# Memory values by tokens: the last four memory-projection tiles of a decode step computed with the tokens stationary, norm weights applied on ScalarE, and cache pages staged later

## The chip, the cores and the metric

The kernel runs on one core of a Trainium2 chip. The metric is the device time of one execution in microseconds; three executions of the kernel before took 619.06, 621.07 and 621.22 us (median 621.07).

The names used below: TensorE (PE in the profile) does the matmuls, PEld is its weight load; VectorE is DVE, ScalarE is ACT, GpSimd is POOL, and SP is the engine that only issues transfers. SP and POOL issue nearly all transfers here; each engine works in the order in which its instructions were written.

## The reference, cut to what matters

One layer of a decoder for 256 prompt tokens and 8 x 4 sampled tokens, all in float32.

```python
def rms_norm(x, g):
    y = xf * lax.rsqrt(jnp.mean(xf * xf, axis=-1, keepdims=True) + NORM_EPS)
    return y * g
...
# memory: 256 tokens x 2048, projected to keys (4 heads x 128) and values (4 heads x 128)
mkv = (rms_norm(mem_prompt, mem_norm_g) @ w_mem_kv).reshape(1, 256, 2, 4, 128)
...
h = rms_norm(x, norm_g)                       # 288 tokens in all
c_h, c_b, c_c, c_g, q, n_g, b_g, kv6, m_q, m_g = split_cols(h @ w_in)
# group A: gated convolution; group B: 8 query heads over compressed, selected and sliding-window
# keys, for the sampled tokens read from 16 cache pages per sequence; group M: attention of m_q
# over the memory keys and values
return x + concatenate([y_a, y_b, y_m]) @ w_out    # and a final rms_norm; mkv is an output too
```

## The kernel before

**Layout and products.** Activations lie with features on the 128 partitions and tokens along the free axis: `x` is 16 planes of 128 x 288, the memory `m` 16 planes of 128 x 256. Every projection runs output tile by output tile: `product` takes a tile of 128 output features, with the weights as stationary operand and the tokens as moving one (matmuls of 256 or 288 columns). A weight tile comes as two halves of 128 x 1024, numbered `s` through the whole program. Float32 accuracy is got from two reduced-precision parts: ScalarE writes a half's high part (`wh`), VectorE its low part (`wl` = `w` - `wh`), and each of the 8 blocks of a half costs three matmuls (high x high, high x low, low x high): 24 in a half, 48 in a tile. `w_hi(s + 2)` and `w_lo(s + 1)` are written when half `s` begins, and `w_load` fetches half `s + 6` near its end into one of five buffers.

**The memory stage.** The 1024 memory columns are 8 tiles: keys are tiles 0 to 3, values 4 to 7. Tiles 0 and 1 go through `first_tiles` on unsplit weights, tiles 2 to 7 through `product` with 256 columns. The reciprocal norms of the tokens (`rstd_m`, held in `Vc`) come late, so they multiply the results. The values are needed with tokens on the partitions, so each value tile is multiplied into `mvt` by VectorE, stored by POOL, and transposed: two transposes into `mvtp` on TensorE and two copies into `mixed` by ScalarE (`mem_rstd`).

**Preparing x.** `x` comes in six pieces `rx` (five of three planes, one of one). `prep_x` multiplies each plane by its norm weights and by the tokens' `rstd_x` on VectorE, three instructions to a piece; ScalarE then writes the piece's high part and VectorE its low part, `x`.

**The cache stream.** Pages are loaded by SP into six buffers `st` as these come free, in one fixed order: compressed pages (`ckc`, multiplied on VectorE and POOL and summed into `pooled`), and in between groups of four tiles of selected keys (`ckk`), which TensorE uses at once (`sk`), later values (`od`). A planner places each use where its own estimate says that the data is there. `window_copies` has POOL issue 16 copies of 512 KB from memory to memory (`o_wk`, `o_wv`), one every `T_WIN[1]` ticks; a tick is half of a weight half. `ON_SYNC` is the half from which weights are issued by POOL and not by SP.

The order of all instructions is written by the program: generators are advanced at every tick by `chunk`. In the profile line L118 is every matmul, L123 every transpose, L135 every VectorE and ScalarE operation.

Of the kernel before, what the change touches and what calls it, by code (L numbers as in the profile page):

```python
# [55 lines left out]
T_MK, T_K1, T_MV, T_V1 = (111, 117), (165, 204), (230, 240), (259, 271)  # L56
T_WIN = (20, 31)
T_LAST = 4
# [6 lines left out]
X_AT = (16, 17)  # L65
ON_SYNC = 14
KV_ORDER = (2, 4, 3, 5, 0, 1)
# [10 lines left out]
def decode_step(ctx, tc, xT, xN, xD, memT, cst, w_in, w_mem, w_out, w_bg, pt, ptv, ckc, ckk, ckv, wk, wv, mk, mv,  # L78
                o_y, o_kv, o_mem, o_conv, o_wk, o_wv):
    nc = tc.nc  # L80
# [163 lines left out]
    def product_half(out, hi, lo, first, last):  # L244
        s = nhalf[0]
        nhalf[0] += 1
        w_hi(s + 2)
        w_lo(s + 1)
        wh, wl = his.pop(s), los.pop(s)
        mm = []  # L250
        for j in range(8):
            a = wh[:, j * 128:(j + 1) * 128]
            mm += [(j, a, hi(j)), (j + (0 if s > DIRECT + 1 else 4), a, lo(j)), (j + 8, wl[:, j * 128:(j + 1) * 128], hi(j))]
        mm.sort(key=lambda x: x[0])
        for n, (_, a, b) in enumerate(mm):
            if s == DIRECT and n == 0:
                w_load(s + WR)
            if n == LOAD_AT:
                w_load(s + WR + 1)
                next(x_next, None)  # L260
            matmul(out, a, b, start=(first and n == 0), stop=(last and n == 23))
            if n == 23 and LOW_FIRST <= s < NH - 18:
                w_lo(s + 2)
            if n % 12 == 11 and not (last and n == 23):
                chunk()
# [3 lines left out]
    def first_tiles():  # L269


        z = [pz.tile([128, 512], F32, name=f"zf{i}", tag="z")[:, :256] for i in range(2)]
        for k0 in (0, 8):
            for i in range(2):
                s = nhalf[0]
                nhalf[0] += 1
                w_hi(s + 2)
                w_lo(s + 1)
                w = raws[s]
                for j in range(8):  # L280
# [470 lines left out]
    for i in range(3):  # L751
# [28 lines left out]

    x_next = x_loads()

    w_load(0)
# [78 lines left out]
    def mem_rstd():  # L862
# [6 lines left out]
        yield 3  # L869
        yield from token_rstd(rstd_m, [macc[:, 0:256]], 256, 1)  # L870
        env["rstd_m"] = True
        for i in range(8):
            while i not in mem_raw:
                yield 1
            dst = mem_raw[i]
            if i < 4:
                vec.tensor_tensor(dst, dst, rstd_m, op=ALU.mult)
            yield 1
            if i == 3:
                nc.gpsimd.dma_start(o_mem[0:4].rearrange("m p n -> p m n"), mkT)  # L880
# [11 lines left out]
    def token_rstd(dst, planes, n, lag):  # L892

# [7 lines left out]
        yield lag  # L901
        r = small(3, "yr")
        w = len(groups)
# [10 lines left out]
    def prep_x():  # L914

        g, r = C("ng"), rstd_x
# [17 lines left out]
    def sum_x():  # L934
# [24 lines left out]
        nc.sync.dma_start(wbg, w_bg)  # L959
        yield 2  # L960
        for t in buffers:
# [38 lines left out]
    def mem_tile(i, z):  # L1000
        dst = mkT[:, i, :] if i < 4 else zt("A", "mvt")[:, :256]
        if i < 4:
            act.activation(dst, z, AF.Copy)
        else:
            yield 2
            assert "rstd_m" in env
            vec.tensor_tensor(dst, z, rstd_m, op=ALU.mult)
        mem_raw[i] = dst

# [529 lines left out]


def _inputs(x_prompt, x_sample, cache_kv, cache_win, state_conv, cache_mem, page_table, mem_prompt,
            norm_g, w_in, w_conv, a_cmp, w_cmp, mem_norm_g, w_mem_kv, w_out, final_g):
# [33 lines left out]
                memT=A(np.concatenate([vec(mem_norm_g), tr(mem_prompt.reshape(256, D)).reshape(128, KT * 256)], 1)), cst=A(cst), w_in=A(_ktiles(wcat)),  # L1576
                w_mem=A(_ktiles(w_mem_kv[0])), w_out=A(_ktiles(wo)), w_bg=A(wbg), pt=A(pt), ptv=A(ptv), ckc=A(ckc), ckk=A(ckk), ckv=A(ckv),
                wk=A(wk), wv=A(wv), mk=A(mk), mv=A(mv))


_OUTS = dict(o_y=(128, KT, NT), o_kv=(12, 128, NT), o_mem=(8, 128, 256), o_conv=(128, 72), o_wk=(4, 2, 128, 1024),
             o_wv=(2, 4, 128, 1024))


def _outputs(r):
# [9 lines left out]
            A(kv[:NTP, 4:6])[None, None], A(conv[0:2])[None, None],  # L1595
            A(r["o_mem"].reshape(2, 4, 128, 256).transpose(3, 0, 1, 2))[None, None],
            A(kv[NTP:, 0:4]).reshape(1, 8, 4, 4, 2, 128), A(win)[None], A(conv[2:18]).reshape(1, 8, 2, 512))
# [15 lines left out]
```

## Time and profile before

| | |
|---|---|
| median of three executions | 621.07 us (619.06 to 621.22) |
| the profiled execution | 622.86 us, its span 620.4 us |
| PE busy | 601.8 us (97% of the span) |
| DVE, ACT, POOL busy | 458.0 (74%), 286.3 (46%), 203.5 us (33%) |
| moved by transfers | 188.40 MB, mean 304 GB/s |

The profiled execution is 1.79 us above the median. Its span leaves 2.46 us of its time around it. Busy time on PE counts overlapping matmuls once; in the timeline view, whose rows give the start, the duration, the engine, the line and the operation, the start of one row and the start of the next say how long the first held the engine.

### The profile page before, as it was taken

Reading aid. Unit: us, or ns where it says so; the run is one execution under the profiler, and the core shown is the slowest. Engines: PE = TensorE matmul, PEld = TensorE weight load, DVE = VectorE, ACT = ScalarE, POOL = GpSimd, SP = SyncE. Lnnn points to the kernel's source line nnn. Section 1 sums busy time; section 2 is a strip of 40 time slices with the busy share of each in tenths; the row PEclk is TensorE's granted clock in tenths of the full one; section 3 lists DMA queues with packets and bytes.
Section 4 is the critical chain, followed back from the end, with each engine's and each line's share of the span. In section 5 each row is a group of like instructions: output and inputs, shape, how many; then the busy total and the mean of one; then the engine's idle time right before and its main releaser. Section 6 shows DMA issues by size and latency. Waiting matters only on the chain.

```text
span 620.4 us, 13332 instructions
## 1 busy us (share of the span) xinstructions
PE 601.8 (97%) x4893; PEld 557.0 (90%) x4893; DVE 458.0 (74%) x737; ACT 286.3 (46%) x500; POOL 203.5 (33%) x282
## 2 busy tenths in 40 slices
PE   8999999999899999999999999999999999999993
PEld 5998999999699998988898888888989889999993
DVE  4789899979395689978978788969586442447764
ACT  4855545444355434335334444344534453446650
POOL 2022545434235334323474522323113434122200
PEclk9999999999999999999999999999999999999997
DMA  8999799999889998978888798899988989578723
GB/s 307 408 406 396 262 329 307 320 314 339 293 264 371 350 408 319 360 278 281 297 288 303 246 375 285 280 345 303 360 296 326 329 283 336 169 252 286 234 89 152
DMA packets 74929, 188.40 MB, mean 304 GB/s; under 512 B 8752, under 2 KB 26064, under 8 KB 74608
## 3 DMA queue, kind: packets, MB, share of 16 engines
q0 software_dynamic: 26048, 100.48, 46.1%
q1 hardware_dynamic: 47664, 85.11, 38.6%
q10 hardware_dynamic: 1152, 1.97, 0.8%
q8 instruction: 38, 0.62, 0.4%
q14 instruction: 27, 0.22, 0.1%
HBM read 182.31 MB, written 13.60 MB: 316 GB/s over the span
## 4 chain that ended last, share of the span: by engine, by line
PE 77%; DVE 10%; DMA 8%; issue 2%; ACT 1%; SPq 0%; ACTq 0%; DVEq 0%
PE z L118 59%; PE od L118 3%; DMA st<-ckk 3%; PE sk L118 3%; DMA st<-ckc 3%; DVE pooled L135 2%; PE zf L118 2%; DVE wl L135 2%; PE acc L118 2%; DMA rx<-xT 2%; PE s L118 2%; DMA mraw<-memT 1%; DVE st L135 1%; PE pt L123 1%; DVE ysum L135 1%
## 5 line engine op out<-in xcount | busy, mean ns | idle before, releaser
L118 PE MATMUL z<-x,wh 128*128 128x288 f32 x1664 | 254.2, 302 | 0.4 <-ACT wh L135 0.4
L135 DVE TENSOR_TENSOR wl<-w,wh 128x1024 fp32r<-128x1024 f32 x148 | 183.9, 1243 | 93.0 <-PE z L118 41.6
L118 PEld LDWEIGHTS z<-x,wh 128*128 128x128 f32 x1664 | 229.4, 188 | 9.2 <-issue 6.9
L135 ACT ACTIVATE wh<-w 128x1024 fp32r<-128x1024 f32 x148 | 154.8, 1052 | 15.8 <-PE z L118 11.7
L118 PE MATMUL z<-x,wl 128*128 128x288 f32 x832 | 127.1, 295 | 0.6 <-DVE wl L135 0.6
L118 PEld LDWEIGHTS z<-x,wl 128*128 128x128 f32 x832 | 115.7, 188 | 0.8 <-DVE wl L135 0.8
L350 POOL TENSOR_TENSOR st<-st,cst 128x512 f32<-128x512 f32 x56 | 62.8, 1121 | 132.9 <-issue 68.2
L219 POOL DMA_DIRECT2D w<-w_in x104 | 58.4, 562 | 91.5 <-DVE wl L135 74.7
L135 DVE TENSOR_REDUCE pooled<-st 128x16 f32<-128x1024 f32 x56 | 67.8, 1210 | 3.4 <-POOL st L350 3.3
L135 DVE TENSOR_TENSOR st<-st,cst 128x512 f32<-128x512 f32 x56 | 40.1, 715 | 4.6 <-DMA st<-ckc 4.3
L572 POOL DMA_INDIRECT st<-ckv,rows_v x29 | 31.2, 1077 | 29.9 <-PE od L118 16.8
L219 POOL DMA_DIRECT2D w<-w_out x32 | 17.5, 550 | 60.1 <-DVE wl L135 43.0
L118 PE MATMUL z<-y,wh 128*128 128x288 f32 x256 | 37.0, 297 | 0.0
L118 PE MATMUL z<-y1a,wh 128*128 128x288 f32 x224 | 35.2, 298 | 0.0
L118 PEld LDWEIGHTS z<-y,wh 128*128 128x128 f32 x256 | 35.1, 188 | 0.0
L118 PEld LDWEIGHTS z<-y1a,wh 128*128 128x128 f32 x224 | 31.5, 188 | 1.6 <-issue 0.8
L118 PE MATMUL z<-m,wh 128*128 128x256 f32 x192 | 27.3, 287 | 0.5 <-DVE mvt L135 0.5
L135 ACT ACTIVATE P<-P,nm 128x128 f32<-128x128 f32 (+1 forms) x32 | 14.2, 445 | 28.1 <-DVE nm L135 28.1
L118 PEld LDWEIGHTS z<-m,wh 128*128 128x128 f32 x192 | 24.7, 191 | 0.8 <-issue 0.7
L118 PE MATMUL sk<-st,qz 128*32 128x256 f32 x288 | 20.5, 382 | 2.5 <-DMA st<-ckk 2.5
L135 ACT ACTIVATE ysum<-z 128x288 f32<-128x288 f32 x16 | 6.6, 413 | 34.1 <-PE z L118 34.1
L118 PE MATMUL z<-y,wl 128*128 128x288 f32 x128 | 19.6, 295 | 0.0
(284 smaller groups left out, 696.4 us busy)
## 6 DMA issues: line engine op xcount, KB each, us to landing
w<-w_in POOLq DMA_DIRECT2D x104, 512.0 KB, 6.4
st<-ckc SPq DMA_DIRECT2D x112, 256.0 KB, 6.5
w<-w_out POOLq DMA_DIRECT2D x32, 512.0 KB, 5.0
st<-ckk SPq DMA_DIRECT2D x112, 128.0 KB, 4.7
w<-w_mem SPq DMA_DIRECT2D x13, 512.0 KB, 7.8
o_wk<-wk POOLq DMA_DIRECT2D x8, 512.0 KB, 6.0
o_wv<-wv POOLq DMA_DIRECT2D x8, 512.0 KB, 6.9
qk<-ckc SPq DMA_DIRECT2D x16, 256.0 KB, 5.4
```

Source lines behind the costliest of these rows:

```text
L118: nc.tensor.matmul(out, a, b, **kw)
L123: nc.tensor.transpose(out, a, b)
L135: return getattr(self.engine, name)(*args, **kw)
L219: (nc.gpsimd if s >= ON_SYNC else nc.sync).dma_start(raws[s], wsrc[s])
L350: done.append(eng.tensor_tensor(tm[:, :, kv], tm[:, :, kv], acmp[:, kv].unsqueeze(1).unsqueeze(1).to_broadcast([128, 2, 4, 64]), op=ALU.mu ...
L572: nc.gpsimd.indirect_dma_start(t, None, ckv, bass.IndirectOffsetOnAxis(ap=rows_v[:, j * 4 + b:j * 4 + b + 1], axis=0))
```

## The change

The four value tiles become `mem_values`: two output tiles `zv0`, `zv1` of 128 tokens x 512 features. The stationary operand is a block of 128 memory tokens (high or low part), the moving one 512 columns of weights, so the matmuls have 512 columns and the result already lies by tokens. The value weights are laid out for it on the host. A token's reciprocal norm is then one number on its partition (`mr`), which ScalarE applies as it copies the result from PSUM; transposes, `mvt` and its copies go. `x`'s norm weights are applied by ScalarE, plane by plane, four halves after the piece was asked for; VectorE then multiplies a whole piece by `rstd_x` in one instruction. `STAGE_AT` lets the pages begin at tick 22 and no sooner (before: 19), `T_WIN` has the copies begin at tick 33 with 30 ticks between (before: 20 and 31), and `ON_SYNC` goes from 14 to 19. `run_half` holds what was the loop of `product_half`.

```diff
-T_WIN = (20, 31)
+T_WIN = (33, 30)
-ON_SYNC = 14
+STAGE_AT = 22
+ON_SYNC = 19
...
+    def run_half(s, mm, last, between=None):
+        m = len(mm) // 2
+        for n, (out, a, b, start, stop) in enumerate(mm):
...
+            if n == LOAD_AT * m // 12:
                 w_load(s + WR + 1)
                 next(x_next, None)
+                if s > 5:
+                    next(x_scale, None)
+            matmul(out, a, b, start=start, stop=stop)
...
+            if n == 7 and between:
+                between()
...
+    def mem_values():
+        z = [pz.tile([128, 512], F32, name=f"zv{tt}", tag="z") for tt in range(2)]
+
+        def out(tt):
+            planes = mixed[:, 12 + 2 * tt:14 + 2 * tt, 0:256]
+            act.activation(planes, z[tt].rearrange("p (a n) -> p a n", a=2), AF.Copy, scale=mr[:, tt:tt + 1])
+            nc.gpsimd.dma_start(o_memv[tt].rearrange("p (a n) -> p a n", a=2), planes)
+
+        for h in range(8):
...
+            for tt in range(2):
+                for k in range(2):
+                    hi, lo = (m_hl[n][:, 2 * h + k, tt * 128:(tt + 1) * 128] for n in range(2))
+                    w = slice(k * 512, (k + 1) * 512)
+                    early = 2 * tt + (k if h == 7 and tt else 0)
+                    mm += [(early, tt, hi, wh[:, w]), (early, tt, lo, wh[:, w]), (2.5 if h == 7 and not tt else 4, tt, hi, wl[:, w])]
...
+        out(1)
...
+    def x_scales():
+        for i in range(6):
+            yield
+            k, t = xg[i]
+            for j in range(t.shape[1] // NT):
+                act.activation(xr[k + j], xr[k + j], AF.Copy, scale=C("ng")[:, k + j:k + j + 1])
...
     def mem_rstd():
...
-            if i >= 4:
-                nc.gpsimd.dma_start(o_mem[i], dst)
-                yield 2
-                t = ptr.tile([128, 512], F32, name=f"mvtp{i}", tag="t")
-                for s in range(2):
-                    transpose(t[:, s * 128:(s + 1) * 128], dst[:, s * 128:(s + 1) * 128], ident)
-                for s in range(2):
-                    act.activation(mvn(s, i - 4), t[:, s * 128:(s + 1) * 128], AF.Copy)
...
     def prep_x():
-                for j in range(k, k + n):
-                    vec.scalar_tensor_tensor(xr[j], xr[j], g[:, j:j + 1], r, op0=ALU.mult, op1=ALU.mult)
+                xv = x.rearrange("p (k n) -> p k n", n=NT)
+                vec.tensor_tensor(xv, xv, r.unsqueeze(1).to_broadcast([128, n, NT]), op=ALU.mult)
...
     def mem_tile(i, z):
-            yield 2
-            assert "rstd_m" in env
-            vec.tensor_tensor(dst, z, rstd_m, op=ALU.mult)
...
-    for i in range(2, 8):
+    for i in range(2, 4):
         then(mem_tile(i, proj(*m_hl, 256)))
+    mem_values()
```

In the instructions the change shows at three places. A name's first number is the half (`w13`) or the tile, the number behind the underscore only tells one use from another.

TensorE in the middle of the value tiles. Before, tile 6 (`z12`, weight half 12), with the two transposes of tile 4 among its matmuls:

```order
L118 MATMUL z12_600<-m1_111,wh12_512 128x256
L118 MATMUL z12_600<-m0_110,wh12_512 128x256
L118 MATMUL z12_600<-m1_111,wh12_512 128x256
L123 MATMUL mvtp4_617<-cst_90,mvt_507 128x128 x2
L118 MATMUL z12_600<-m0_110,wh12_512 128x256
L118 MATMUL z12_600<-m1_111,wh12_512 128x256
L118 MATMUL z12_600<-m0_110,wh12_512 128x256
L118 MATMUL z12_600<-m1_111,wh12_512 128x256
L118 MATMUL z12_600<-m0_110,wl12_558 128x256 x8
```

Now, the second part of one half and the beginning of the next, on the two token tiles:

```order
L119 MATMUL zv1_426<-wh10_427,m0_110 128x512
L119 MATMUL zv1_426<-wh10_427,m1_111 128x512
L119 MATMUL zv0_425<-wl10_460,m0_110 128x512 x2
L119 MATMUL zv1_426<-wl10_460,m0_110 128x512 x2
L119 MATMUL zv0_425<-wh11_458,m0_110 128x512
L119 MATMUL zv0_425<-wh11_458,m1_111 128x512
L119 MATMUL zv0_425<-wh11_458,m0_110 128x512
L119 MATMUL zv0_425<-wh11_458,m1_111 128x512
```

A half is 12 matmuls of 512 columns where it was 24 of 256, and the transposes are gone. In all, 192 matmuls of 256 columns and 8 transposes go and 96 matmuls of 512 come; every other matmul stays.

VectorE from the moment that both sets of reciprocal norms are there. Before (`mixed` is a key tile, `Vc` the norms):

```order
L135 TENSOR_TENSOR mixed_95<-mixed_95,Vc_99 128x256 x2
L135 SCALAR_TENSOR_TENSOR rx0_247<-rx0_247,cst_90,rstd_x_117 128x288 x3
L135 TENSOR_TENSOR wl10_467<-w10_281,wh10_423 128x1024
L135 TENSOR_TENSOR mixed_95<-mixed_95,Vc_99 128x256
L135 SCALAR_TENSOR_TENSOR rx_283<-rx_283,cst_90,rstd_x_117 128x288 x3
L135 TENSOR_TENSOR mixed_95<-mixed_95,Vc_99 128x256
L135 TENSOR_TENSOR x1_113<-rx0_247,x0_112 128x864
L135 TENSOR_TENSOR wl11_514<-w11_316,wh11_465 128x1024
L135 SCALAR_TENSOR_TENSOR rx_283<-rx_283,cst_90,rstd_x_117 128x288 x3
L135 TENSOR_TENSOR mvt_507<-z8_422,Vc_99 128x256
L135 TENSOR_TENSOR x1_113<-rx_283,x0_112 128x864
L135 TENSOR_TENSOR wl12_558<-w12_355,wh12_512 128x1024
```

Now:

```order
L136 TENSOR_TENSOR mixed_95<-mixed_95,Vc_99 128x256 x2
L136 TENSOR_TENSOR rx0_248<-rx0_248,rstd_x_118 128x864
L136 TENSOR_TENSOR wl10_460<-w10_282,wh10_427 128x1024
L136 TENSOR_TENSOR mixed_95<-mixed_95,Vc_99 128x256
L136 TENSOR_TENSOR rx_284<-rx_284,rstd_x_118 128x864
L136 TENSOR_TENSOR mixed_95<-mixed_95,Vc_99 128x256
L136 TENSOR_TENSOR x1_113<-rx0_248,x0_112 128x864
L136 TENSOR_TENSOR wl11_486<-w11_317,wh11_458 128x1024
L136 TENSOR_TENSOR rx_284<-rx_284,rstd_x_118 128x864
L136 TENSOR_TENSOR x1_113<-rx_284,x0_112 128x864
L136 TENSOR_TENSOR wl12_518<-w12_356,wh12_484 128x1024
```

Three instructions to a piece have become one, and `mvt` is gone; what follows what is the same.

ScalarE over the same stretch, now (before, the rows on `rx` were not there):

```order
L136 ACTIVATE wh9_384<-w9_258 128x1024
L136 ACTIVATE rx0_248<-rx0_248,cst_90 128x288 x3
L136 ACTIVATE mixed_95<-z6_325 128x256
L136 ACTIVATE rstd_x_118<-rx_420 128x288
L136 ACTIVATE wh10_427<-w10_282 128x1024
L136 ACTIVATE Vc_99<-ssq_342 128x256
L136 ACTIVATE rx_284<-rx_284,cst_90 128x288 x3
L136 ACTIVATE x0_112<-rx0_248 128x864
L136 ACTIVATE wh11_458<-w11_317 128x1024
```

Each group of three stands ahead of a weight half's high part and waits for a piece of `x` to land.

In POOL's order the third copy, an `o_wk`, stood behind the transfer of weight half 46 and now stands behind that of half 51. On TensorE the first group of selected keys (`sk`) stood behind 504 matmuls of 288 columns and the second behind 660; now they stand behind 576 and 696. The last value group (`od`) stood behind 2736 and now stands behind 2760, of 3264.

More of the change, by code (lines that the diff above doesn't have):

```diff
@@ L78, in decode_step @@
 def decode_step(ctx, tc, xT, xN, xD, memT, cst, w_in, w_mem, w_out, w_bg, pt, ptv, ckc, ckk, ckv, wk, wv, mk, mv,
-                o_y, o_kv, o_mem, o_conv, o_wk, o_wv):
+                o_y, o_kv, o_mem, o_memv, o_conv, o_wk, o_wv):
     nc = tc.nc
@@ L254, in product_half @@
         mm.sort(key=lambda x: x[0])
-        for n, (_, a, b) in enumerate(mm):
+        run_half(s, [(out, a, b, first and n == 0, last and n == 23) for n, (_, a, b) in enumerate(mm)], last)
+    def run_half(s, mm, last, between=None):
+        m = len(mm) // 2
+        for n, (out, a, b, start, stop) in enumerate(mm):
             if s == DIRECT and n == 0:
                 w_load(s + WR)
-            if n == LOAD_AT:
+            if n == LOAD_AT * m // 12:
                 w_load(s + WR + 1)
                 next(x_next, None)
-            matmul(out, a, b, start=(first and n == 0), stop=(last and n == 23))
-            if n == 23 and LOW_FIRST <= s < NH - 18:
+                if s > 5:
+                    next(x_scale, None)
+            matmul(out, a, b, start=start, stop=stop)
+            if n == 2 * m - 1 and LOW_FIRST <= s < NH - 18:
                 w_lo(s + 2)
-            if n % 12 == 11 and not (last and n == 23):
+            if n == 7 and between:
+                between()
+            if n == m - 1:
+                chunk()
+            if n == 2 * m - 1 and not last:
                 chunk()
@@ L299, in first_tiles @@
                     yield z[i]
+    def mem_values():
[5 more added lines that the diff above has]
+        for h in range(8):
+            s = nhalf[0]
+            nhalf[0] += 1
+            w_hi(s + 2)
+            w_lo(s + 1)
+            wh, wl = his.pop(s), los.pop(s)
+            mm = []
+            for tt in range(2):
[4 more added lines that the diff above has]
+                    mm += [(early, tt, hi, wh[:, w]), (early, tt, lo, wh[:, w]), (2.5 if h == 7 and not tt else 4, tt, hi, wl[:, w])]
+            mm.sort(key=lambda x: x[0])
+            i = [[n for n, x in enumerate(mm) if x[1] == tt] for tt in range(2)]
+            run_half(s, [(z[tt], a, b, h == 0 and n == i[tt][0], h == 7 and n == i[tt][-1]) for n, (_, tt, a, b) in enumerate(mm)],
+                     h == 7, (lambda: out(0)) if h == 7 else None)
+        assert "rstd_m" in env
+        out(1)
+        chunk()
     def proj(hi, lo, N):
@@ L757, in decode_step @@
     rstd_m = Vc
+    mr = one.tile([128, 2], F32, name="mr")
     rstd_x = zt("C", "rstd_x")
@@ L869, in mem_rstd, with token_rstd @@
         yield 3
[L870 removed]
+        yield from token_rstd(rstd_m, [macc[:, 0:256]], 256, 1, mr)
         env["rstd_m"] = True
[L872 removed]
+        for i in range(4):
             while i not in mem_raw:
                 yield 1
[L875 to L877 removed]
+            vec.tensor_tensor(mem_raw[i], mem_raw[i], rstd_m, op=ALU.mult)
             yield 1
[L879 to L888 removed]
+        nc.gpsimd.dma_start(o_mem.rearrange("m p n -> p m n"), mkT)
     GROUPS = ((0, 0), (128, 0), (160, 96))
[L892 removed]
+    def token_rstd(dst, planes, n, lag, r):
         groups = [x for x in GROUPS if x[0] + 128 <= n]
@@ L901, in token_rstd @@
         yield lag
-        r = small(3, "yr")
         w = len(groups)
@@ L914, in prep_x @@
     def prep_x():
-        g, r = C("ng"), rstd_x
+        r = rstd_x
         flat = lambda t, k, n: t[:, k:k + n, :].rearrange("p k n -> p (k n)")
@@ L959, in sum_x @@
         nc.sync.dma_start(wbg, w_bg)
-        yield 2
+        while now[0] < STAGE_AT:
+            yield 1
         for t in buffers:
@@ L1000, in mem_tile @@
     def mem_tile(i, z):
[L1001 to L1005, printed above, removed]
-            assert "rstd_m" in env
-            vec.tensor_tensor(dst, z, rstd_m, op=ALU.mult)
-        mem_raw[i] = dst
+        act.activation(mkT[:, i, :], z, AF.Copy)
+        mem_raw[i] = mkT[:, i, :]
+        return
+        yield
     cos, sin = C("cos"), C("sin")
@@ L1538, in _ktiles, with _kpairs @@
     return w.reshape(KT, 128, n, 128).transpose(2, 1, 0, 3).reshape(n, 128, KT * 128)
+def _kpairs(w):
+    return w.reshape(4, 4, 128, 512).transpose(0, 2, 1, 3).reshape(4, 128, 2048)
 def _inputs(x_prompt, x_sample, cache_kv, cache_win, state_conv, cache_mem, page_table, mem_prompt,
@@ L1576, in _inputs @@
                 memT=A(np.concatenate([vec(mem_norm_g), tr(mem_prompt.reshape(256, D)).reshape(128, KT * 256)], 1)), cst=A(cst), w_in=A(_ktiles(wcat)),
-                w_mem=A(_ktiles(w_mem_kv[0])), w_out=A(_ktiles(wo)), w_bg=A(wbg), pt=A(pt), ptv=A(ptv), ckc=A(ckc), ckk=A(ckk), ckv=A(ckv),
+                w_mem=A(np.concatenate([_ktiles(w_mem_kv[0][:, :512]), _kpairs(w_mem_kv[0][:, 512:])])), w_out=A(_ktiles(wo)), w_bg=A(wbg), pt=A(pt), ptv=A(ptv), ckc=A(ckc), ckk=A(ckk), ckv=A(ckv),
                 wk=A(wk), wv=A(wv), mk=A(mk), mv=A(mv))
-_OUTS = dict(o_y=(128, KT, NT), o_kv=(12, 128, NT), o_mem=(8, 128, 256), o_conv=(128, 72), o_wk=(4, 2, 128, 1024),
+_OUTS = dict(o_y=(128, KT, NT), o_kv=(12, 128, NT), o_mem=(4, 128, 256), o_memv=(2, 128, 512), o_conv=(128, 72), o_wk=(4, 2, 128, 1024),
              o_wv=(2, 4, 128, 1024))
```

3 lines of the change are left out of this document (2 added, 1 removed).

## Prediction

> **What bounds the kernel now.** I read the page first, then who waited for whom on TensorE, then the busy time by stages, then the timeline of TensorE, VectorE and ScalarE around the memory stage.
>
> ```profile
> span 620.4 us, 13332 instructions
> PE 601.8 (97%) x4893; PEld 557.0 (90%) x4893; DVE 458.0 (74%) x737; ACT 286.3 (46%) x500; POOL 203.5 (33%) x282
> ```
>
> TensorE is busy 97% of the span. What is left is 18.6 us, most of it ahead of the first matmuls and behind the last; so time can be won where TensorE has less to do, or where it stands still in between. Where it stands still:
>
> ```profile
> PE sk L118 <- DMA st<-ckk: 2.5, 2, 1.7
> PE z L118 <- DVE mvt L135: 0.5, 1, 0.5
> ```
>
> Only these two bear on the change: a wait for cache pages, and one for VectorE to empty a PSUM tile of memory values. By stages (columns: stretch, then the busy time of PE, PEld, DVE, ACT, POOL with instruction counts, the granted clock, the transfer share, GB/s):
>
> ```profile
> 40.00:50.00 10.00, 10.00 (x86) 10.00 (x85) 10.00 (x18) 5.42 (x6) 3.46 (x6) 1.00 1.03 399
> 50.00:60.00 10.00, 9.50 (x88) 8.86 (x90) 10.00 (x16) 6.00 (x11) 2.98 (x6) 1.00 1.04 400
> 150.00:160.00 10.00, 8.04 (x67) 6.34 (x65) 5.85 (x8) 4.09 (x9) 1.97 (x4) 1.00 1.01 377
> ```
>
> In the memory stage VectorE is full too, and the transfers run at 400 GB/s. There TensorE is fed just in time; at 150 to 160 us it waits for pages, with VectorE half idle. The clock is at full speed in all three.
>
> **The change part by part.**
>
> *Narrow matmuls into wide ones.* TensorE's rows around the value tiles and in the x stage:
>
> ```profile
> 40.64 2.08 PE L118 MATMUL z<-m,wh 128*128 128x256 f32 x16
> ...
> 43.52 2.08 PE L118 MATMUL z<-m,wh 128*128 128x256 f32 x16
> ...
> 46.40 1.60 PE L118 MATMUL z<-m,wh 128*128 128x256 f32 x12
> 47.85 0.38 PE L123 MATMUL mvtp<-cst,mvt 128*128 128x128 f32 x2
> ...
> 49.50 2.08 PE L118 MATMUL z<-m,wh 128*128 128x256 f32 x16
> ...
> 53.08 1.66 PE L118 MATMUL z<-m,wh 128*128 128x256 f32 x12 [0.50 <-DVE mvt L135]
> ...
> 59.19 2.15 PE L118 MATMUL bg<-rx,qmz 128*32 128x288 f32 x32
> ...
> 78.70 2.29 PE L118 MATMUL z<-x,wh 128*128 128x288 f32 x16
> ...
> 81.90 2.29 PE L118 MATMUL z<-x,wh 128*128 128x288 f32 x16
> ```
>
> From 40.64 to 43.52 one half of 24 matmuls passes: 2.88 us, 0.120 us each. In the x stage 3.20 us for 24, 0.1333 us each. The 32 further columns cost 13.3 ns, 0.417 ns a column, so a matmul is its columns plus a fixed 13.3 ns. A matmul of 512 columns is then 0.2267 us. 192 x 0.120 = 23.04 us become 96 x 0.2267 = 21.76 us: **-1.28 us**. The trace has hardly a matmul of this kind with 512 columns; the nearest are four over 96 rows:
>
> ```profile
> 281.95 0.41 PE L118 MATMUL acc<-pcT,vcp 96*128 96x512 f32 x1
> 282.20 1.05 PE L118 MATMUL s<-qk,qq 128*128 128x128 f32 x8
> ```
>
> Here 0.25 us pass until the next one, with a change of kind in it, which the value tiles lack. At that price 96 cost 24.0 us, 0.96 us more than now; with the columns alone (0.2133 us) they cost 20.5 us, 2.56 us less. I take 1.28, since it follows from the kind's own two widths.
>
> The Trainium skill (TensorE: Matmul & The Clock Gate, section Back-to-back issue gap) gives a sustained spacing for streams of weight load and matmul of about 131 ns at 512 columns. By it the 96 would take 12.6 us. The trace speaks against it: 288 columns already take 133 ns here. It is a rival below.
>
> *Transposes.* The half with a transpose pair runs from 46.40 to 49.50 us, 3.10 instead of 2.88: 0.22 us for two transposes. Four pairs: **-0.88 us**, all on TensorE, which has no slack there. The copies of them on ScalarE and `mvt` on VectorE go too; they lie beside TensorE.
>
> *The wait for `mvt`.* **-0.50 us**: the accumulators are held through all eight halves, so VectorE no longer empties a PSUM tile in that stretch. What replaces it is ScalarE's copy of `zv0`, written ahead of the last four value matmuls (0.9 us); the first x product needs that buffer. At the 0.45 us that ScalarE takes for 288 columns (row below) 512 are at most 0.8, so it just fits.
>
> *VectorE and ScalarE between the tiles.*
>
> ```profile
> 37.63 1.37 DVE L135 SCALAR_TENSOR_TENSOR rx<-rx,cst,rstd_x 128x288 f32<-128x288 f32 x3
> 38.92 1.22 DVE L135 TENSOR_TENSOR wl<-w,wh 128x1024 fp32r<-128x1024 f32 x1
> 40.05 0.42 DVE L135 TENSOR_TENSOR mixed<-mixed,Vc 128x256 f32<-128x256 f32 x1
> ...
> 42.01 1.05 DVE L135 TENSOR_TENSOR x<-rx,x 128x864 fp32r<-128x864 f32 x1
> 42.98 1.22 DVE L135 TENSOR_TENSOR wl<-w,wh 128x1024 fp32r<-128x1024 f32 x1
> ...
> 45.41 0.41 DVE L135 TENSOR_TENSOR mvt<-z,Vc 128x256 f32<-128x256 f32 x1
> 45.74 1.04 DVE L135 TENSOR_TENSOR x<-rx,x 128x864 fp32r<-128x864 f32 x1
> ```
>
> Start to start: three `rx` 1.29 us, a `wl` 1.13, an `x` 0.97, an `mvt` 0.33. An elementwise instruction on 864 columns is 0.97, so each full `rx` piece saves 0.32 and all of it about 1.6 + 4 x 0.33 = 2.9 us of VectorE. A half with one piece costs VectorE 1.13 + 0.97 + 0.97 = 3.07 us from now on (3.39 before, 3.72 with `mvt`). TensorE's half shrinks from 2.88 to 12 x 0.2267 = 2.72 us. So VectorE still falls behind, by 0.35 us a half where it was 0.51 to 0.84. I walked it from 37.63 us: `wl14` is done at 53.1 and its first matmul is due at 52.8; `wl15` is done at 55.55 and due at 55.4 with that shift. The last low part of `x`, at 56.0, is ahead of its use. So short waits for `wl` replace the one for `mvt`: **+0.4 us**, between 0 and 1.
>
> ScalarE gets the 16 scalings. The same operation stands in the last stage, the other two of a half at 49 us:
>
> ```profile
> 49.24 0.93 ACT L135 ACTIVATE x<-rx 128x864 fp32r<-128x864 f32 x1 [1.84 <-DVE rx L135]
> 50.07 1.04 ACT L135 ACTIVATE wh<-w 128x1024 fp32r<-128x1024 f32 x1
> 51.02 0.42 ACT L135 ACTIVATE mixed<-mvtp 128x128 f32<-128x128 f32 x2
> ...
> 575.25 0.54 ACT L135 ACTIVATE ysum<-ysum,cst 128x288 f32<-128x288 f32 x1
> 575.70 1.05 ACT L135 ACTIVATE wh<-w 128x1024 fp32r<-128x1024 f32 x1
> ...
> rx<-xT SPq DMA_DIRECT2D x5, 432.0 KB, 9.6
> ```
>
> Start to start a scaling is 0.45 us, 7.2 us in all, in a stretch where ScalarE works 5.4 to 6.0 us in 10. A half then asks of it 1.35 (three scalings), 0.83 (`x`'s high part) and 0.95 (`wh`): 3.13 us in 2.72. It starts ahead by two halves, and in the walk `wh14` is ready 0.3 us before TensorE wants it; nothing is added, but the cover is thin. The scaling waits for a piece to land, with the next `wh` queued behind it. A piece is asked for four halves (10.9 us) ahead and took 9.6 us, so this wait is nil unless transfers get slower; they get lighter, since pages and the first copy no longer run beside them.
>
> *Queues.* Weight halves 14 to 18 are issued by SP. Each waits there for its buffer, and the last piece of `x` and the first pages stand behind them. The stores of the values wait on POOL for ScalarE's copies, with half 21 queued behind the first. It is issued near 57 us and TensorE wants it past 70. Zero for both; the cover is the five weight buffers.
>
> *Pages later.* SP begins with them at 36.94 us now, and will behind half 16, which waits for `wl11`, near 43.7. The uses shift by 24 to 72 matmuls (3.2 to 9.6 us) against the products. The stream's end has room:
>
> ```profile
> 36.94 61.92 SPq L336 DMA_DIRECT2D st<-ckc  x32
> ...
> 533.74 1.86 PE od L118 x32
> ...
> L135 ACT ACTIVATE ysum<-z x16: 411/413/413, 497.5 to 555.1; 128x288 f32<-128x288 f32 x16
> ```
>
> The last value group is at 533.74 and the first output pass ends at 555, so 3.2 us more are hidden. What isn't hidden is the wait for the second group of selected keys:
>
> ```profile
> 130.67 1.93 PE L118 MATMUL sk<-st,qz 128*32 128x256 f32 x32
> ...
> 143.86 1.02 PE L118 MATMUL sm<-mixed,qk 128*128 128x256 f32 x4
> 144.53 0.89 PE L118 MATMUL z<-x,wh 128*128 128x288 f32 x4
> ...
> 147.92 0.51 POOL L692 DMA_DIRECT2D o_wk<-wk  x1
> ...
> 160.55 1.02 PE L118 MATMUL sk<-st,qz 128*32 128x256 f32 x10 [1.70 <-DMA st<-ckk]
> ...
> 163.75 1.78 PE om L118 x16
> ```
>
> Its pages landed 29.9 us after the first group began, since buffers come free only by then. Between the groups there will be 120 matmuls of `z` instead of 156 (-4.8 us), but two `sm` more (2 x 0.67), an `om` (1.78) and a `ptm` (four transposes, 0.44): TensorE arrives 1.3 us sooner, and the wait of 2.46 us would be 3.8. Against it, the copy at 147.92 us, 1 MB of reading and writing at 377 GB/s, 2.8 us, moves behind this group: 1.0. I put it midway, no change: **0**, between -2.5 and +1.3.
>
> **Sum:** -1.28 - 0.88 - 0.50 + 0.4 + 0 = -2.3 us. The profiled execution of 622.86 would be 620.6, its span 618.1. That one stands 1.79 above the median; on the median of 621.07 the forecast is 618.8 us, 0.37% faster. About 0.5%, 3.1 us, is what a measurement of this kernel can tell from no change.
>
> **The rivals.**
> - *The wait for pages goes as well.* For it: the copy is out of the way. Against: TensorE comes sooner. 618.8 - 2.5 = 616.3 us.
> - *VectorE and ScalarE become the pace of the value halves.* Both need some 3.1 us a half against TensorE's 2.72; if the lead of the first halves is not there (a piece of `x` late at the first scaling), all eight halves run at 3.1: 8 x 0.37 = 3.0 in place of 0.4, 621.4 us. The sum of both engines' rows speaks for it, the walk against.
> - *Wide matmuls cost 0.25 us*, as in the one row at 281.95: 618.8 + 2.2 = 621.0 us.
> - *Slower: page groups meet copies.* The ten groups of keys are planned by estimates, and the sixteen copies fall at other places. A group that needs its pages while a copy runs waits 2.8 us, as at 150 us. One such wait more gives 621.6; from two on it is decided, 624.4 us.
> - *Wide matmuls at about 0.13 us*: the chip would stream 512 columns in the time of 288. 96 x 0.096 = 9.2 us less, 609.6. The two widths of this trace speak against it. The page named above is its only support.
>
> **How the numbers follow.** The forecast has 0.45, the page wait gone 0.20, the slow pace 0.17, dear wide matmuls 0.07, two waits for copies 0.09, cheap wide matmuls 0.02. The forecast's own spread is about 1.2 us, from the waits and the widths. Faster than 617.97: all of 0.20, a quarter of 0.45, and 0.02: 0.34. Slower than 624.2: most of 0.09, so 0.08. The rest, 0.58, is within 0.5%. The range from 615.6 to 621.9 takes in the page wait gone and the slow pace, and leaves out the two copies and the cheap matmuls.
>
> **What the changed profile would show.** Value matmuls of 512 columns 0.227 us apart, 2.72 us a half; no `mvtp`; the value matmuls over near 57.4 us, where `bg` begins at 59.19 now (two of the four transpose pairs lie behind it); waits of TensorE for `wl` or `wh` under 1 us before 60 us; the wait for `ckk` at the second `sk` between 1 and 4 us. The prediction is wrong if value halves take 3 us or more, if `rx` scalings hold up a `wh`, or if new waits for `st` stand behind 100 us.

## The result and the profile after

The changed kernel takes 624.92 us (median of seven executions, 624.05 to 628.0); the kernel before, run beside it and earlier, 620.32 us (seven, 618.42 to 621.28). The ratio is 1.0092, with a 95% interval of 1.0072 to 1.0111: slower by some 5.7 us (the two medians are 4.6 us apart), where 618.8 us and 0.4% faster were forecast.

The page of the kernel after, its head and the busy times:

```profile
span 622.9 us, 13111 instructions
PE 604.1 (97%) x4789; PEld 553.4 (89%) x4789; DVE 455.6 (73%) x723; ACT 293.0 (47%) x510; POOL 202.4 (32%) x275
```

TensorE has 104 matmuls and transposes fewer and is busy 2.3 us longer: part of its waiting inside the groups of selected keys counts as busy here, as the holds below show. TensorE's timeline in the memory stage (start, duration, engine, line, operation):

```profile
37.78 2.00 PE L119 MATMUL zv<-wh,m 128*128 128x512 f32 x8
39.61 1.07 PE L119 MATMUL zv<-wl,m 128*128 128x512 f32 x4
40.52 1.98 PE L119 MATMUL zv<-wh,m 128*128 128x512 f32 x8
42.33 1.07 PE L119 MATMUL zv<-wl,m 128*128 128x512 f32 x4
43.24 1.98 PE L119 MATMUL zv<-wh,m 128*128 128x512 f32 x8
...
51.40 1.98 PE L119 MATMUL zv<-wh,m 128*128 128x512 f32 x8
53.40 1.20 PE L119 MATMUL zv<-wl,m 128*128 128x512 f32 x4
54.43 1.52 PE L119 MATMUL zv<-wh,m 128*128 128x512 f32 x6
...
57.39 1.86 PE L119 MATMUL z<-x,wh 128*128 128x288 f32 x12
59.18 1.18 PE L119 MATMUL bg<-rx,qmz 128*32 128x288 f32 x16
```

A half takes 2.72 us (40.52 to 43.24), 0.2267 us a matmul, and the first product of `x` begins at 57.39 us. (`bg`, which stood ahead of it, now stands behind twelve of its matmuls.) The fourth half of the x stage begins at 70.27 us where it began at 72.29: 2.0 us are won. By stages, the same stretches as before:

```profile
40.00:50.00 10.00, 10.00 (x45) 8.28 (x45) 9.83 (x11) 9.08 (x15) 0.83 (x1) 1.00 1.00 361
50.00:60.00 10.00, 9.97 (x59) 7.40 (x62) 8.38 (x10) 8.07 (x11) 3.45 (x6) 1.00 0.94 329
```

VectorE is still nearly full, ScalarE has gone from 5.42 to 9.08 us in 10, the transfers carry 361 GB/s instead of 399, and TensorE stands still nowhere. So the stage is not where the time went. Who waited for whom on TensorE, us in total, times, longest:

```profile
PE sk L119 <- DMA st<-ckk: 1.8, 2, 1.6
PE sk L119 <- DMA qk<-ckk: 1.7, 2, 1.3
PE z L119 <- ACT y1a L136: 1.7, 1, 1.7
```

The wait for pages is still there but in other groups, and one for `y1a` is new (part of the input of the first output tile, which ScalarE writes from the memory attention's result). TensorE's timeline at the fourth and the ninth group of selected keys and at the first output tile:

```profile
206.93 1.48 PE L119 MATMUL sk<-st,qz 128*32 128x256 f32 x18
208.62 0.62 PE L119 MATMUL sk<-st,qz 128*32 128x256 f32 x2 [0.21 <-DMA st<-ckk]
210.58 0.59 PE L119 MATMUL sk<-qk,qz 128*32 128x256 f32 x2 [1.34 <-DMA qk<-ckk]
211.52 0.38 PE L119 MATMUL sk<-qk,qz 128*32 128x256 f32 x1 [0.35 <-DMA qk<-ckk]
...
212.60 1.86 PE L119 MATMUL z<-x,wh 128*128 128x288 f32 x12
...
443.63 0.76 PE L119 MATMUL sk<-st,qz 128*32 128x256 f32 x6
445.98 1.02 PE L119 MATMUL sk<-st,qz 128*32 128x256 f32 x10 [1.59 <-DMA st<-ckk]
...
490.89 1.30 PE L119 MATMUL z<-y1a,wh 128*128 128x288 f32 x8
493.85 0.93 PE L119 MATMUL z<-y1a,wh 128*128 128x288 f32 x4 [1.66 <-ACT y1a L136]
```

A group of 32 whose pages are there holds TensorE 1.86 us, and the fourth holds it 5.27 (from its first row to the next of another kind, added over its rows, without the 16 small `sc` between them). The brackets tell less than the hold: in the fourth group they add up to 1.90 us, and the hold is 3.41 us longer than 1.86. SP's queue for that fourth group, before and then after:

```profile
190.09 13.01 SPq L336 DMA_DIRECT2D st<-ckk  x16
203.88 0.86 SPq L336 DMA_DIRECT2D qk<-ckc  x2
...
210.45 1.93 PE L118 MATMUL sk<-st,qz 128*32 128x256 f32 x32
```

```profile
190.77 10.19 SPq L378 DMA_DIRECT2D st<-ckk  x12
201.73 3.13 SPq L378 DMA_DIRECT2D qk<-ckk  x4
```

From the first page's issue to the use there were 20.4 us (20.1 in a second profile of before), and now there are 16.2. Besides, the last four of the sixteen now go to the buffer called `qk`, and are issued only from 201.73 on, when the other twelve have been issued.

The end of that queue says most. Before, the last page's issue was over 7.3 us ahead of the use (203.11 to 210.45; 8.6 us in the second profile); now it is 2.1 us (204.86 to 206.93). By the trace these four pages took 7.2 to 8.5 us to land. The last, begun at 204.2, took 7.2 and was there at 211.4, and TensorE went on at 211.52. The ninth group is the same case: its last page was issued at 439.6 us and took 6.2, TensorE came at 442.74 and went on at 445.98.

From the start of that fourth half to the first `rb`, a matmul of the final norm, TensorE needs 539.4 us where it needed 534.6, 4.75 us more. Second group 5.49 to 1.87: -3.6; fourth 1.75 to 5.27: +3.5; ninth 1.76 to 4.19: +2.4; `y1a`: +1.7; together +4.0, with 0.75 scattered. The 2.0 us of the memory stage come off that: +2.7, and the span is 2.5 us longer. The medians differ by some 2 us more, since that execution of before was a long one: a second profile of it has no wait at the second group (e4 below). Against that second profile the account is simpler. It needs 532.3 us for the same way, 7.1 us less than now; the groups (+6.0) and `y1a` (+1.7) are all of that and 0.5 us more. The memory stage gives 1.9 us back, and the span is 5.0 us longer (622.9 and 617.9).

### The profile page after: what moved, and what is told of

It reads as the page before. It is cut to its first block, busy times and chain, and to the rows that moved or that the text cites. A ratio compares the mean times of both kernels' runs of the same rounds, so it can differ in the third digit from the quotient of the medians.

```text
span 622.9 us, 13111 instructions
## 1 busy us (share of the span) xinstructions
PE 604.1 (97%) x4789; PEld 553.4 (89%) x4789; DVE 455.6 (73%) x723; ACT 293.0 (47%) x510; POOL 202.4 (32%) x275
## 3 DMA queue, kind: packets, MB, share of 16 engines
q10 hardware_dynamic: 1152, 1.97, 0.9%
## 5 line engine op out<-in xcount | busy, mean ns | idle before, releaser
L392 POOL TENSOR_TENSOR st<-st,cst 128x512 f32<-128x512 f32 x54 | 61.1, 1133 | 124.8 <-DVE st L136 67.1
L220 POOL DMA_DIRECT2D w<-w_in x101 | 56.9, 564 | 100.4 <-DVE wl L136 72.0
L136 DVE TENSOR_REDUCE pooled<-st 128x16 f32<-128x1024 f32 x54 | 65.3, 1210 | 8.1 <-POOL st L392 8.1
L614 POOL DMA_INDIRECT st<-ckv,rows_v x30 | 34.0, 1134 | 41.5 <-PE od L119 22.7
L136 DVE TENSOR_TENSOR st<-st,cst 128x512 f32<-128x512 f32 x54 | 37.0, 686 | 9.6 <-DMA st<-ckc 9.6
L136 ACT ACTIVATE se<-z 128x288 f32<-128x288 f32 x16 | 6.6, 411 | 42.9 <-PE z L119 42.9
L119 PE MATMUL z<-y1a,wl 128*128 128x288 f32 x128 | 19.5, 294 | 0.0
```

What stands on the lines that cost most here:

```text
L119: nc.tensor.matmul(out, a, b, **kw)
L136: return getattr(self.engine, name)(*args, **kw)
L220: (nc.gpsimd if s >= ON_SYNC else nc.sync).dma_start(raws[s], wsrc[s])
L392: done.append(eng.tensor_tensor(tm[:, :, kv], tm[:, :, kv], acmp[:, kv].unsqueeze(1).unsqueeze(1).to_broadcast([128, 2, 4, 64]), op=ALU.mu ...
L614: nc.gpsimd.indirect_dma_start(t, None, ckv, bass.IndirectOffsetOnAxis(ap=rows_v[:, j * 4 + b:j * 4 + b + 1], axis=0))
```

## The experiments

They follow in the order in which they were run. Three theories were held in turn: that the new numbers or the copies cost the time, that the stream keeps its own pace and swallows any lead, and at last that single groups come ahead of their pages. The expectations show which was held when. A ratio is always to the kernel before on the same chip.

**e1: the three numbers back.** The kernel after with

```diff
-T_WIN = (33, 30)
+T_WIN = (20, 31)
-STAGE_AT = 22
-ON_SYNC = 19
+STAGE_AT = 19
+ON_SYNC = 14
```

> The changed kernel with the three staging numbers of before: pages from tick 19, copies from tick 20 every 31, weights on SP up to half 13. Theory A (the late pages cost the time: key groups wait, and the first output pass waits for the memory attention of the sampled tokens): the gain of the memory stage stays, 1.8 to 2.2 us, and most of the loss goes, so 617 to 621 us, 0.99 to 1.00 of before; TensorE waits under 2.5 us for ckk in all and not at all for y1a. Rival B (any new order of the stream costs it, or the values and scalings themselves do): 623 to 626 us as the changed kernel.

623.6 us, ratio 1.0045 (1.0028 to 1.0062). About half of the loss goes with the numbers; the rest stays, and the memory stage's gain does not show.

**e2: only the value tiles.** e1, with `x`'s norm weights on VectorE again:

```diff
-                xv = x.rearrange("p (k n) -> p k n", n=NT)
-                vec.tensor_tensor(xv, xv, r.unsqueeze(1).to_broadcast([128, n, NT]), op=ALU.mult)
+                for j in range(k, k + n):
+                    vec.scalar_tensor_tensor(xr[j], xr[j], g[:, j:j + 1], r, op0=ALU.mult, op1=ALU.mult)
```

> Memory values by tokens alone, norm weights of x on VectorE and the staging numbers as before. Theory A: like e1 within 1 us, since the scalings lie off TensorE's path; VectorE is busier before 60 us, so waits for wl of up to 1 us more. Rival C (the scalings on ScalarE cost or save something of weight): differs from e1 by over 1.5 us.

626.63 us, 1.0092 (1.0059 to 1.0125). So the scalings on ScalarE cost nothing that shows; without them the x stage comes 1.5 us later (its fourth half begins at 71.25 us, in e1 at 69.77). The order of TensorE's groups is that of e1, and yet the second group holds it 4.94 us and the fourth 3.51 here, 1.87 and 1.97 in e1. The last pages of these two groups are issued 2.9 and 3.9 us ahead of the use here, 4.6 and 4.9 us in e1.

**e3: only the three numbers, on the kernel before.**

```diff
-T_WIN = (20, 31)
+T_WIN = (33, 30)
-ON_SYNC = 14
+STAGE_AT = 22
+ON_SYNC = 19
...
-        yield 2
+        while now[0] < STAGE_AT:
+            yield 1
```

> The kernel before with the three new staging numbers and nothing else. Theory A: slower than before by 3 to 7 us (623 to 627), with waits for ckk in key groups and for the first output pass. Rival B: the same as before within 1 us, since the memory stage is as it was.

627.45 us, 1.0105 (1.0082 to 1.0128). The numbers alone cost the kernel before as much as the whole change does.

**e4: the kernel before again**, unchanged, one execution with its profile:

> The kernel before, unchanged, for a second profile. Theory A, with the wait of 2.5 us for the second key group belonging to the one slow profiled execution (622.86 against a median of 620.3): span 617 to 619 us with a wait for ckk under 1 us. Rival: the wait is there in every execution, 2 to 3 us.

619.68 us. The second group, in the timeline of e4:

```profile
155.61 1.93 PE L118 MATMUL sk<-st,qz 128*32 128x256 f32 x32
```

All 32 in one row and no wait. The 2.46 us that the prediction reckoned with are not in every execution of the kernel.

**e5: another order on the kernel before.** The planner's estimate of a transfer's delay, half a microsecond longer:

```diff
-DMA_PIECE, DMA_LAG = 1.75, 4.0
+DMA_PIECE, DMA_LAG = 1.75, 4.5
```

> The kernel before with one number of the planner raised (the delay that it adds to every transfer, 4.0 to 4.5 us), so that its stream takes nearly the order that e1 has: key groups behind 516, 672, 816, 948, 1068 matmuls (e1: 528, 672, 816, 948, 1068; before: 504, 660, 804, 948, 1056), memory attention out behind 2460, value groups behind 2520 to 2760 in both. No instruction is added or removed. Theory D (the order of the stream that follows from the shorter memory stage costs what the stage saves): slower than before by 2 to 5 us, 623 to 626. Rival E (what is left of the loss in e1 comes from the values and scalings): the same as before within 1.5 us.

622.08 us, 1.0041 (1.0021 to 1.0062), with the groups nearly where e1 has them (behind 516, 672, 816, 948 and 1068 matmuls; e1 528, 672, 816, 948, 1068). By the medians the order alone costs as much as e1 loses. Its profile, of its shortest execution, does not show where: no group waits in it, and of TensorE's other waits one for a `wl` at 244.76 us has grown, from 0.55 us in e4 to 2.10.

**e6: only `STAGE_AT` back**, copies and queues as changed.

```diff
-STAGE_AT = 22
+STAGE_AT = 19
```

> The changed kernel with pages from tick 19 again, copies and weight queue as changed; TensorE's order is that of e1. If the tick alone makes the staging loss: as e1, 1.003 to 1.006 of before. If the copies or the weights on SP make it: as the changed kernel, 1.007 to 1.011.

620.53 us, 1.0018 (0.9994 to 1.0041). The three ticks are most of the loss, 0.7 of 0.9% (on two chips). The copies and the queues do no harm: e1, with the old ones, stands at 1.0045 (on another chip, and the intervals overlap, so a gain from them is not shown).

**e7: pages sooner, old copies and queues.**

```diff
-T_WIN = (33, 30)
+T_WIN = (20, 31)
-STAGE_AT = 22
-ON_SYNC = 19
+STAGE_AT = 17
+ON_SYNC = 14
```

> The changed kernel with pages from tick 17, the earliest that the program reaches, and copies and weight queue of before. Key groups then stand behind 516, 672, 804, 924, 1044 matmuls and the last value group behind 2712. Theory A (late pages cost): faster than e1 by 1 to 3 us and not slower than before, 0.995 to 1.002. Rival: pages then crowd out x and weights in the memory stage, waits for wh or wl there, slower than e1.

622.86 us, 1.0042 (1.0017 to 1.0068). In the profiled execution, a long one of 627.2 us, TensorE waits 1.6 us for a `wh` among the value tiles and begins `bg` at 63.20 us (e6 58.98).

**e8: no copies.** The kernel after without the sixteen copies, whose outputs stay unwritten:

```diff
-    spawn(window_copies(), 3)
```

> The changed kernel without the sixteen window copies, so its window outputs are not written; order of TensorE as changed. If contention with the copies makes the waits of key groups: 3 to 6 us less than the changed kernel, 0.998 to 1.004 of before. If the place of the groups makes them: within 2 us of the changed kernel, 1.006 to 1.010.

626.05 us, 1.0091 (1.0057 to 1.0126): taking away 16.8 MB of traffic changes nothing. The fourth group in the timeline of e8:

```profile
209.29 1.49 PE L119 MATMUL sk<-st,qz 128*32 128x256 f32 x20
212.88 0.59 PE L119 MATMUL sk<-qk,qz 128*32 128x256 f32 x2 [2.10 <-DMA qk<-ckk]
214.45 0.38 PE L119 MATMUL sk<-qk,qz 128*32 128x256 f32 x1 [0.97 <-DMA qk<-ckk]
```

The same group waits for the same buffer, 5.83 us held. The copies are not what it waits for: its last four pages took 7.5 to 9.1 us to land without them, 7.2 to 8.5 with them.

**e9, e10 and e12: the lead taken back.** Ahead of the first x matmul that matmul is written 17 times more (35 in e12); the planner and every order stay. e9 and e12 on e6, e10 on the kernel before.

```diff
+            if s == 16 and n == 0:
+                for _ in range(17):
+                    nc.tensor.matmul(out, a, b, start=True, stop=True)
```

> The kernel after with STAGE_AT at 19 (e6) and, ahead of the first x matmul, 17 more matmuls of 288 columns that write what that matmul writes again: 17 x 0.1333 = 2.27 us of TensorE at the end of the memory stage, which gives back what the memory stage gained; planner and orders are those of e6. Theory (the gain of the memory stage is used up by waits for the stream, which runs at its own pace): at most 0.7 us above e6, ratio to before 1.000 to 1.004, and the first-half groups of selected keys start at e6's times to within 1 us. Rival (the gain lasts to the end, and what eats it are new costs of the change elsewhere): 2.27 us above e6, ratio 1.0055.

> The kernel before with the same 17 repeated matmuls ahead of the first x matmul. Theory: the stream's pages have some 1 to 2 us of room in the order of before (its own spread between executions is 2 to 3 us), so 0 to 1 us slower, ratio 1.000 to 1.002. Rival (TensorE alone sets the time): +2.27 us, ratio 1.0037.

> As e9 with 35 repeats: 35 x 0.1333 = 4.67 us of TensorE ahead of the first x matmul, more than the memory stage gained. Theory: the room of the stream is used up, part of it shows: 1 to 3 us above e6, ratio 1.004 to 1.007. Rival (TensorE alone sets the time): +4.67, ratio 1.0093.

e9: 625.42 us, 1.0063 (1.0037 to 1.0089), against e6's 1.0018, on another chip, some 2.8 us for 2.27 us of matmuls. e12: 626.95 us, 1.0102 (1.0057 to 1.0147), 5.2 us for 4.67. e10: 622.16 us, 1.0018 (0.9994 to 1.0043), 1.1 us at the median; between the profiles of e4 and e10 every group moves by 2.1 to 2.3 us, and so does the span (617.9 and 620.1). The theory that the stream swallows a lead falls: TensorE's lead lasts to the end. The fourth group, in the timelines of e6, e9 and e12:

```profile
206.51 1.50 PE L119 MATMUL sk<-st,qz 128*32 128x256 f32 x22
209.08 0.81 PE L119 MATMUL sk<-st,qz 128*32 128x256 f32 x9 [1.07 <-DMA st<-ckk]
```

```profile
207.26 1.50 PE L119 MATMUL sk<-st,qz 128*32 128x256 f32 x22
209.66 0.81 PE L119 MATMUL sk<-st,qz 128*32 128x256 f32 x9 [0.91 <-DMA st<-ckk]
```

```profile
210.32 1.50 PE L119 MATMUL sk<-st,qz 128*32 128x256 f32 x22
213.37 0.81 PE L119 MATMUL sk<-st,qz 128*32 128x256 f32 x9 [1.54 <-DMA st<-ckk]
```

TensorE comes up to 3.8 us later and waits no less. So the pages are late by the order, not by the clock: the issue of the group's last page moves along with TensorE, over at 202.20, 203.18 and 206.31 us. Begun at 201.7, 202.8 and 205.9 us, these pages took 7.2, 6.7 and 7.3 to land: 208.9, 209.5 and 213.2 us, and TensorE goes on at 209.08, 209.66 and 213.37. That their buffers come free later because their users stand in the same order fits this, and was not tested by itself.

**e11: pages sooner, new copies and queues.** The kernel after with

```diff
-STAGE_AT = 22
+STAGE_AT = 17
```

> The kernel after with STAGE_AT at 17, copies and ON_SYNC as changed: the groups of selected keys stand behind 516, 672, 804, 924 and 1044 matmuls, near before's 504, 660, 804, 948 and 1056, the last value group behind 2712 instead of 2736. Theory (the place of the groups alone makes the loss, and the stream has its own pace): no gain over e6, ratio 0.998 to 1.003. Rival (with the groups back in their places the memory stage's 2 us come out): ratio 0.996 to 0.998. If pages crowd the weight halves as in e7 (a wait for wh in the value halves), above 1.003.

621.43 us, 0.9999 (0.9968 to 1.0029). No wait for `wh` as in e7, but in its profiled execution, a long one of 623.65 us, the first group holds TensorE 3.45 us and the fourth 4.35.

**e13 and e14: the planner told to come later, `STAGE_AT` 22.** The kernel after; e14 has 3.0 for 1.0.

```diff
-            while (... or at[0] < ready[u, j]
+            while (... or at[0] < ready[u, j] + (1.0 if u is selk_use else 0)
```

> The kernel after, with the planner told to put a group of selected keys 1 us later than its estimate says. That moves the fourth group from behind 960 to behind 972 matmuls, the seventh, eighth and ninth from 2052, 2148, 2232 to 2064, 2172, 2244, and leaves the others and the memory attention (2496) where they are. Theory (the loss of after is in groups that come ahead of their pages: its ten groups hold TensorE 24.4 us where 18.4 are the work): the fourth group's 5.27 us become about 3.7 and the ninth's 4.19 about 2.6, some 3 us less, ratio to before 1.004 to 1.006. Rival (the stream moves later as a whole, and a later use frees its buffer later): no better than after, 1.008 to 1.011.

> The same with 3 us: groups behind 600, 720, 876, 1008, 1116 and 1980, 2100, 2208, 2292, 2340 matmuls. Theory: no group waits any more, the ten hold TensorE 18.4 to 19 us, only the wait for y1a (1.7 us) stays: 6 us less than after, ratio 0.999 to 1.003. Rival: waits come back at other groups or at the values, ratio 1.007 or more.

e13: 622.53 us, 1.0032 (1.0009 to 1.0055), 3.7 us less than after for four groups moved by 12 or 24 matmuls. The fourth holds 2.75 us instead of 5.27, the ninth 1.75 instead of 4.19. e14: 625.78 us, 1.009 (1.0057 to 1.0123), no better than after: later is no cure by itself. Its fourth group, moved by 48 matmuls, holds 5.16 us, and TensorE waits 2.5 us for `wl`.

**e15 and e16: the same with 2.0**, on e6 (`STAGE_AT` 19) and on the kernel before.

> The kernel after with STAGE_AT at 19 (e6) and a margin of 2 us for groups of selected keys: behind 540, 684, 840, 972, 1080 and 1932, 2040, 2148, 2220, 2280 matmuls (e6: 528, 672, 816, 948, 1068 and 1908, 2016, 2124, 2220, 2280). Theory: the fourth group's wait (3.25 us held where 1.86 is the work, in e6) goes, and the memory stage's gain of 2 us comes out: ratio 0.995 to 0.999. Rival (some group waits whatever the margin, since the transfers are the limit there): 1.001 or more.

> Control: the kernel before with the same margin of 2 us, groups behind 528, 672, 828, 960, 1068 and 1932, 2040, 2136, 2220, 2268 matmuls (before: 504, 660, 804, 948, 1056 and 1908, 2016, 2124, 2196, 2256). Theory: before hardly waits at its groups (18.4 us in its second profile, 22.05 in its first), so the margin gives at most its occasional wait back: 0.996 to 1.001. Rival (every other order than before's costs, as e5's did): 1.003 to 1.006.

e15: 617.2 us, 0.9949 (0.9931 to 0.9968), faster than both kernels. Its fourth group, SP's queue and TensorE's timeline:

```profile
189.18 11.38 SPq L378 DMA_DIRECT2D st<-ckk  x16
201.74 0.86 SPq L378 DMA_DIRECT2D qk<-ckc  x2
...
208.18 1.93 PE L119 MATMUL sk<-st,qz 128*32 128x256 f32 x32
```

From the first page's issue to the use pass 19.0 us (20.4 before, 16.2 after, 17.1 in e6), all sixteen pages go to `st`, and nothing waits. The last page's issue is over 7.6 us ahead of the use (e6: 4.3 us and a page that takes 7.2 to land; e5: 4.2 us, pages that take 5.3, and no wait). e16: 625.99 us, 1.0083 (1.0062 to 1.0103): on the kernel before the same margin makes waits at its second group (2.97 us) and eighth (3.99), and it waits 2.11 us for a `wl`; the profiled execution is the longest of its seven, 631.39 us. A margin is no rule; on one kernel it made an order that fits, on the other one that does not.

**e17 and e18: whose gain is it?** e15 with the 17 repeated matmuls of e9, and e15 again, on one chip.

> The kernel of e15 with 17 repeated matmuls (2.27 us of TensorE) ahead of the first x matmul: it takes back what the memory stage gained and keeps every order. Theory (e15's gain is the memory stage's, which comes out where no group waits): +2 us against e15, ratio to before 0.997 to 1.000. Rival (e15's gain is all in the better places of the groups): within 0.7 us of e15, ratio 0.994 to 0.996.

> The kernel of e15 once more, beside e17 on the same chip: the version that beat both kernels. If e15 was no accident, ratio 0.993 to 0.997; an accident would give 1.000 or more.

e18: 617.53 us, 0.9937 (0.9918 to 0.9955). e17: 620.29 us, 0.9981 (0.9961 to 1.0001). The 2.27 us cost 2.8: where no group waits, the memory stage's lead comes out in full, and the rest of e18's gain, about 1.2 us by e17 (an interval that just reaches nothing), is the places of the groups.

All of them together. "Held" is what the ten groups of selected keys held TensorE in the profiled execution, 1.75 to 1.87 us each where nothing waits:

| kernel | held, us | groups over 2 us | ratio |
|---|---|---|---|
| before, two profiles | 22.05 and 18.38 | second 5.49; none | 1 |
| after | 24.36 | 4th 5.27, 9th 4.19 | 1.0092 |
| e1, e2, e3 | 19.59, 24.36, 21.23 | 8th; 1st, 2nd, 4th, 8th; 2nd, 3rd, 9th | 1.0045, 1.0092, 1.0105 |
| e5, e10 | 18.51, 18.40 | none | 1.0041, 1.0018 |
| e6, e9, e12 | 20.92, 21.70, 20.87 | 2nd, 4th, 6th; 4th, 6th; 4th, 9th | 1.0018, 1.0063, 1.0102 |
| e7, e8, e11 | 22.94, 23.25, 23.06 | 1st, 2nd, 4th, 7th; 1st, 4th; 1st, 4th, 9th | 1.0042, 1.0091, 0.9999 |
| e13, e14 | 19.39, 22.80 | 4th; 1st, 4th | 1.0032, 1.0090 |
| e15, e17, e18 | 18.64, 18.66, 18.66 | none | 0.9949, 0.9981, 0.9937 |
| e16 | 21.85 | 2nd, 8th | 1.0083 |

The held time is of one execution and the ratio of many: the profiles of e1 and e5 are of their shortest executions (620.53 and 620.18 us, medians 623.6 and 622.08) and those of e7, e11 and e16 of long ones (627.2, 623.65 and 631.39 us, medians 622.86, 621.43 and 625.99). The table also leaves out every other wait of TensorE. So it shows where groups wait, and a ratio can't be worked out from it: e11 holds 23.06 us at 0.9999, e5 18.51 at 1.0041.

## Why the prediction was wrong, step by step

- **Wide matmuls, -1.28: right.** 0.2267 us each, 2.72 us a half. The rival of about 131 ns that came from the Trainium skill (TensorE: Matmul & The Clock Gate, section Back-to-back issue gap) does not hold for these matmuls: the trace has 0.2267 us at 512 columns, as the kind's two narrower widths said.
- **Transposes, -0.88, and the wait for `mvt`, -0.50: right.** Both are gone, and the first x product begins at 57.39 us, forecast 57.4.
- **New waits for `wl`, +0.4: about right.** The last two halves take 3.03 and 2.96 us instead of 2.72, 0.55 us together; the page of waits names none there. The stage's net of -2.26 us measured -2.0.
- **ScalarE and the queues, 0: right.** No `wh` is late; e2, with the scalings back on VectorE, was no faster.
- **The wait for the second group, taken as unchanged: wrong in its footing.** It is gone after, but e4 does not have it either. A wait of one profiled execution was taken for a property of the kernel, and the forecast of 1 to 4 us there failed.
- **Pages later, 0: this step failed.** It was judged by the end of the stream, where the last value group has 21 us of room, and by one group out of ten. The other nine were not held against their pages. Two of them came too soon, +3.5 and +2.4 us, and the memory attention of the sampled tokens, behind 2496 matmuls instead of 2448, came to stand right ahead of the first output tile, which then waited 1.7 us for `y1a`. The orders showed all three places; the prediction did not look. Against the second profile of before, the groups and `y1a` together are 7.6 us where the term had 0. Going back from tick 22 to 19 takes away 4.6 us of the loss (e6) and still does not give the forecast: the shorter memory stage alone also moves the groups (the first three stand behind 528, 672 and 816 matmuls in e6, behind 504, 660 and 804 before), and the fourth then holds TensorE 3.25 us. Only with the groups placed anew does the gain come out (e15, e18).
- **The slower rival** ended at 624.4 us, near the 624.92 measured, but by another mechanism: it had the groups meet copies, and e8 shows that without the copies the same time is lost. So that nearness is luck. Shown are: the three ticks of `STAGE_AT` are most of the loss (e6, e3), groups that come ahead of their pages are where TensorE stands (the holds, e13), and the memory stage's gain is real and lasts (e9, e12, e17).

Of the signs named ahead, the value halves, `mvtp`, the 57.4 us and the waits before 60 us came as forecast. The wait at the second `sk`, forecast between 1 and 4 us, did not come. The new waits for `st` behind 100 us, named as what would make it wrong, are what happened.

What stays open: why SP issues a group's last pages as late as it does in a given order (in after and e8 four of them go to `qk`, in e6 none does), and why later in e2 than in e1, whose order it has; where the median of e5 loses its time; and what the wait for `y1a` alone costs, since no run took it away by itself. It stands in every profile with `STAGE_AT` at 22 (1.28 us in e3, 1.65 or 1.66 in after, e8, e13 and e14) and in no other.

## What to carry to other kernels

A saving on a full engine is worth its size only if what that engine meets later is not tied to where it stands: when a stage gets shorter, hold every later just-in-time use against its transfer, each by its own rows, and not the last one for all. Numbers that set an order are tuned for one timing; after any change they are to be searched again, and here the same change went from 0.9% slower to 0.5 or 0.6% faster by two of them, `STAGE_AT` and the planner's margin (e15, e18). And profile the kernel twice before reckoning with a wait: what one execution shows, the next may not.

## What the runs showed of the hardware

Coming later on TensorE did not let late pages catch up: the fourth group waited 1.07, 0.91 and 1.54 us when TensorE came to it at 206.51, 207.26 and 210.32 us (e6, e9, e12). The executions of e6 spread by 5.5 us (618.42 to 623.95), those of e15 and e18, the same kernel but for the places of the groups, by 1.9 us (616.75 to 618.64, 17 executions). That this steadiness comes from the places is not shown: e17, with the same places, spreads by 3.1 us (619.03 to 622.1). How long a page of 128 KB takes to land is not one number: the last one of the fourth group took 7.2 us in after and 9.1 in e8. And the copies, 16.8 of some 196 MB read and written, cost nothing that can be measured (e8).
